# Ten of twelve adaLN modulation vectors: from 512-column matmuls to row sums on three engines

## The chip, the cores and the metric

One Trainium2 chip, one core. The metric is device microseconds (us) of one execution of the whole program; lower is better. Three runs of the kernel before gave 2099.13 us in the median (2097.63 to 2105.65).

## What is computed

Two layers of a diffusion backbone over 512 latent and 256 context tokens of width 1024, all in float32. Before every sub-layer the tokens are normalised and modulated by vectors that depend on the sample alone. Per layer `l` there are six vectors of 1024 numbers (shift, scale and gate of the mixer, then of the experts), each in two variants: from `c` for the latents and from `c_ctx` for the context.

```python
mods  = jnp.split(silu_c  @ ada_w[l] + ada_b[l], 6, axis=-1)   # latents
modsc = jnp.split(silu_cc @ ada_w[l] + ada_b[l], 6, axis=-1)   # context
```

`ada_w[l]` is 1024 x 6144, so one vector (layer `l`, number `m`) needs a 1024 x 1024 block of weights, 4 MB, read once. Twelve such blocks are read in all; the change is about ten of them. After the modulations of a mixer come attention heads, an output projection, a router and 16 experts.

## The kernel before

The weights arrive in tiles with 128 rows of `ada_w` on the 128 partitions. The product with the two silu vectors sums over rows, so over partitions and over eight tiles. `csil` holds the silu vectors as columns: `csil[:, k, 0:2]` belongs to the rows of tile `k`, and 30 further columns are zero.

**Where the modulations are computed.** `ada_first` (L183) makes vectors 0 and 1 of layer 0 at the very start; it isn't changed. The other ten come out of `ada(l, g, ...)` (L217 to L256), five generators that each make two vectors. One has a pool of two 1 MB tiles (`aw`, L403) and loads two tiles ahead (L221, on SP's queue). Each of its eight steps `k` issues four matmuls (L234), with 32 stationary columns and 512 moving columns each, into four quarters of the partitions of one PSUM tile `ps_ada`. After the eighth step VectorE adds the bias (L239), TensorE transposes the row (L244), VectorE copies to `modT` (L248) and makes `Asc` (L252), and GpSimd's queue writes the gates to DRAM (L256).

**How the work is interleaved.** Layer 0's mixer starts with a stage, some 60 to 360 us, in which the projections of the heads (`job`, L516, made of `proj_t`, L474, and `proj_v`, L499), the differential attention (`diff_head`, L651) and the generators of `ada` run together. Generators stand in two queues: `fill` takes the projections, `fill2` takes `ada`. `run_fill(n)` (L612) steps them: every third turn steps `fill2`, the others step `fill`.

- `dense(4); drain()` (L548): the first four projection jobs, q and k of head 0 with 12 steps each, and two value jobs of 24 steps each, 72 steps in all.
- For each of four heads `dense(2)` (24 steps), the `ada` generators of that head (L552), and `diff_head`, whose `weave` makes 26 turns of `run_fill`.
- `dense(2); drain(True)` (L561): two value jobs for the neighbourhood heads, and whatever `ada` has left. Then `st_a.close()` gives `aw`'s memory to the pool `p0n` of the neighbourhood attention (L564).

**What sets the order on an engine.** The program is written in this order, but a planner orders each engine's instructions anew, with earlier code first among what it takes to be ready. A tile of a pool waits for the release of an earlier tile of the same tag. Projections, `ps_ada` and `ps_adat` share the PSUM tag "mm", which has two buffers (L397); scores have the tag "S", transposes "tr", attention outputs "pv". Each engine and each DMA queue (SP's, ACT's, GpSimd's) runs its list in order.

Of the kernel before, what the change touches and what calls it, by code (L numbers as in the profile page):

```python
# [10 lines left out]
F32 = mybir.dt.float32  # L11
# [3 lines left out]
AF = mybir.ActivationFunctionType  # L15
OP = mybir.AluOpType
# [4 lines left out]
D = 1024  # L21
# [107 lines left out]
def _build(tc, a, out, dump=None, upto=99):  # L129
# [6 lines left out]
    with ExitStack() as root:  # L136
# [77 lines left out]
                        ada_ins[8] = V.scalar_tensor_tensor(Asc[0][0][:, v, ks], modT[0][:, 1, v, ks], 1.0, norm_t[:, 0, ks], op0=OP.add, op1=OP.mult)  # L214
                    yield

        def ada(l, g, csil, wp, pp, sm):  # L217

            def load(k):
                w = wp.tile([P, 2048], F32, name="w_ada", tag="w")  # L220
                Y.dma_start(w, a["ada_w"][l, k * P:(k + 1) * P, g * 2048:(g + 1) * 2048])  # L221
                return w

            br = wp.tile([P, 512], F32, name="adab", tag="br", bufs=1)
            bsrc = a["ada_b"][l:l + 1, g * 2048:(g + 1) * 2048]
            S.dma_start(br, bass.AP(bsrc.tensor, bsrc.offset, [[512, 4], [0, 32], [1, 512]]))
            depth = 2
            ws = deque(load(k) for k in range(depth))
            yield
            ps = pp.tile([P, 512], F32, name="ps_ada", tag="mm")  # L230
            for k in range(8):
                w = ws.popleft()
                for j in range(4):
                    T.matmul(ps[32 * j:32 * j + 32, :], csil[:, k, :], w[:, j * 512:(j + 1) * 512], start=(k == 0), stop=(k == 7))  # L234
                if k + depth < 8:
                    ws.append(load(k + depth))
                yield
            row = sm.tile([P, 512], F32, name="mrow", tag="t2k", bufs=T2K)
            V.tensor_tensor(row, ps, br, op=OP.add)  # L239
            yield  # L240
            yield
            pt = pp.tile([P, 4, P], F32, name="ps_adat", tag="mm")
            for c4 in range(4):
                T.transpose(pt[:, c4, :], row[:, c4 * P:(c4 + 1) * P], ident)  # L244
            for c4 in range(4):
                src = pt[:, c4, :].rearrange("p (jh jl q) -> p jh jl q", jh=2, jl=2)[:, :, :, 0:2]
                dst = modT[l][:, 2 * g:2 * g + 2, :, c4::4].rearrange("p m v jl -> p m jl v")
                V.tensor_copy(dst, src)  # L248
            for s in range(2):
                if 1 + 3 * s in (2 * g, 2 * g + 1):  # L250
                    for v in range(2):
                        V.scalar_tensor_tensor(Asc[l][s][:, v, :], modT[l][:, 1 + 3 * s, v, :], 1.0, norm_t[:, 2 * s + l, :], op0=OP.add, op1=OP.mult)  # L252
            if g:
                for half in range(2):
                    j = 2 * (g - 1) + half
                    G.dma_start(garow[l][g - 1, :, half * 512:(half + 1) * 512], row[32 * j:32 * j + 2, :])  # L256

        def rstd_pow(dst, ssq, n):
            G.tensor_scalar(dst, ssq, 1.0 / n, EPS, op0=OP.mult, op1=OP.add)
# [135 lines left out]
        def mix0(st, st_h, wu, stage):  # L395
# [4 lines left out]
            bp = st.enter_context(tc.tile_pool(name="p0b", bufs=1, reuse_waits="tile"))  # L400
            sm = st.enter_context(tc.tile_pool(name="p0s", bufs=2, reuse_waits="tile"))
            st_a = ExitStack()
            aw = st_a.enter_context(tc.tile_pool(name="p0aw", bufs=2, reuse_waits="tile"))  # L403
            csil = lo.tile([P, 8, 32], F32, name="csil", tag="csil")
            S.dma_start(csil, a["cp"])
            S.dma_start(ident, a["ident"])
            S.dma_start(norm_t, a["norm_t"])
            S.activation(csil, csil, AF.Silu)
            hh = hx.tile([P, 8, 768], F32R, name="hh", tag="hh")
            hl = hx.tile([P, 8, 768], F32R, name="hl", tag="hl")  # L410

# [26 lines left out]
                if n == UNIT0:  # L438
                    prep(0)

            with tc.tile_pool(name="p0ax", bufs=2, reuse_waits="tile") as ax:
                first = ada_first(csil, [aw, ax], pp, sm, between)
                for g in range(2):
                    next(first)
                    if g == 0:
                        for i in range(6):
                            S.activation(junk, xt[i], AF.Square, accum_out=ssq[:, i:i + 1])
                        rstd_pow(ssq, ssq, D)
                        for i in range(6):
                            V.tensor_scalar(xt[i], xt[i], ssq[:, i:i + 1], None, op0=OP.mult)  # L450
                    for k in range(4 * g, 4 * g + 4):
                        pt = pp.tile([P, 8, P], F32, name="ps_h", tag="S")
                        for i in range(6):
# [81 lines left out]
            def dense(n):  # L535

                for _ in range(n):
                    fill.append(job(cur[0]))
                    cur[0] += 1


            with tc.tile_pool(name="p0d", bufs=2, reuse_waits="tile") as dp:
                rope = dp.tile([P, 2, LX], F32, name="rope0", tag="rope0", bufs=1)
                with after[0], after[1], after[2]:
                    Y.dma_start(rope, a["rope0"])
                    prep(1)
                rope_of["r"] = rope
                dense(4)  # L548
                drain()
                for h in range(4):  # L550
                    dense(2)
                    for g in (((0, 1),), ((0, 2),), ((1, 0),), ((1, 1), (1, 2)))[h]:  # L552
                        fill2.append(ada(*g, csil, aw, pp, sm))
                    diff_head(h, qk["q", "d", h], qk["k", "d", h], vv, nlam, cT, pp, sm, dp)
                    drain()
                    run_late()
# [46 lines left out]
        def step(q):  # L603
            while q:
                try:
                    next(q[0])
                    return True
                except StopIteration:
                    q.popleft()
            return False  # L610

        def run_fill(n):  # L612

            while n > 0:
                turn[0] += 1
                if turn[0] % 3 == 0:
                    step(fill2)
                elif step(fill):
                    n -= 1
                elif not step(fill2):  # L620
                    return
                else:
                    n -= 2

        def drain(both=False):
            while fill:
# [1158 lines left out]
```

## Time and profile before

| what | value |
|---|---|
| median of three runs | 2099.13 us |
| the profiled execution's own time | 2102.01 us |
| its span, first to last instruction | 2100.2 us |
| busy: TensorE (PE), VectorE (DVE), ScalarE (ACT), GpSimd (POOL) | 93%, 38%, 22%, 11% of the span |
| share of the chain that ended last | PE 79%, DMA 9%, DVE 6% |
| mean granted TensorE clock | 0.976 |

Busy time of PE counts matmuls whose ends are modelled and which overlap one another, so a busy PE is not one at its peak. PEld is the weight load that goes with a matmul. A float32 matmul shows as two records, so four matmuls of a step show as eight. The chain is followed back from the last instruction to what released each step. In rows with `[idle <- X]` the engine stood idle so long before the instruction, until X let it go.

### The profile page before, as it was taken

The numbers are of one execution on the slowest core, as the hardware profiler recorded it, in microseconds if no ns is written. First come the engines' busy times: TensorE is split into PE (matmuls) and PEld (weight loads), VectorE is DVE, ScalarE is ACT, GpSimd is POOL, SyncE is SP. The second block draws the span as 40 slices with busy tenths as digits, with TensorE's granted clock in tenths as the row PEclk, the third lists the DMA queues.
The fourth block names the chain that finished last, engine by engine and source line by source line (L and its number), as shares of the span: only waits on it lengthen the run. The fifth ranks groups of instructions, "written<-read, shape, count | busy, mean of one in ns | idle before, by whom it ended". The sixth has DMA issues, their size and how long they took to land.

```text
span 2100.2 us, 26868 instructions
## 1 busy us (share of the span) xinstructions
PE 1961.1 (93%) x11092; PEld 1044.3 (50%) x11092; DVE 787.7 (38%) x1719; ACT 459.9 (22%) x881; POOL 234.4 (11%) x205
## 2 busy tenths in 40 slices
PE   5899999997979999999999899999969999999997
PEld 1765567875763333333333598455654334443342
DVE  2445553555562322223232741666561121121112
ACT  3233431344330000000000522455320000000002
POOL 1201111112321000000000210101300000000000
PEclk9999999999979999999999999999979999999999
DMA  8354446212667999999999622100278999999965
GB/s 264 121 184 167 171 169 221 64 64 97 216 233 291 355 392 385 397 384 396 386 398 383 175 61 85 66 1 21 106 290 320 389 409 394 375 388 410 388 257 202
DMA packets 174738, 528.81 MB, mean 252 GB/s; under 512 B 11368, under 2 KB 51624, under 8 KB 169496
## 3 DMA queue, kind: packets, MB, share of 16 engines
q1 hardware_dynamic: 162160, 487.75, 61.2%
q0 software_dynamic: 7712, 26.91, 4.6%
q10 hardware_dynamic: 4744, 12.44, 1.9%
q8 instruction: 87, 1.43, 0.3%
q14 instruction: 35, 0.29, 0.0%
HBM read 511.56 MB, written 14.71 MB: 251 GB/s over the span
## 4 chain that ended last, share of the span: by engine, by line
PE 79%; DMA 9%; DVE 6%; ACT 3%; issue 2%; POOL 2%; SPq 0%; ACTq 0%; DVEq 0%; POOLq 0%
DMA moe_w<-in_moe_w 6%; PE ps_a L1125 6%; PE ps_c L173 5%; PE ps_b L1125 5%; PE ps_d L1331 5%; PE ps_d L173 4%; PE ps_a L173 3%; PE ps_b L173 3%; PE ps_x L1318 3%; PE ps_c L1344 3%; PE ps_px L323 3%; PE ps_ada L234 3%; PE ps_e L173 2%; PE ps_px L324 2%; PE ps_px L325 2%; PE ps_s L1737 2%
## 5 line engine op out<-in xcount | busy, mean ns | idle before, releaser
L1125 PE MATMUL ps_b<-moe_w,xeT 128*64 128x512 f32 x512 | 183.2, 597 | 0.0
L1125 PE MATMUL ps_a<-moe_w,xeT 128*64 128x512 f32 x512 | 177.2, 598 | 4.1 <-DVE xeT L1321 3.5
L1127 ACT ACTIVATE hid<-ps_a 128x512 f32<-128x512 f32 x32 | 19.1, 597 | 616.7 <-PE ps_a L1125 401.8
L1128 DVE TENSOR_TENSOR hid<-hid,ps_b 128x512 f32<-128x512 f32 x32 | 22.0, 688 | 313.6 <-PE ps_b L173 149.9
L173 PE MATMUL ps_a<-moe_w,xeT 128*64 128x512 f32 x512 | 139.6, 598 | 0.0
L173 PE MATMUL ps_b<-moe_w,xeT 128*64 128x512 f32 x512 | 137.7, 593 | 0.0
L173 PE MATMUL ps_d<-moe_w,hidT 128*64 128x512 f32 x512 | 114.8, 594 | 3.8 <-DMA moe_w<-in_moe_w 3.6
L173 PE MATMUL ps_c<-moe_w,xeT 128*32 128x512 f32 x1024 | 114.9, 601 | 0.0
L1331 PE MATMUL ps_d<-moe_w,hidT 128*64 128x512 f32 x448 | 102.2, 595 | 0.0
L1125 PEld LDWEIGHTS ps_b<-moe_w,xeT 128*64 128x64 f32 x512 | 54.1, 137 | 74.3 <-issue 68.9
L1125 PEld LDWEIGHTS ps_a<-moe_w,xeT 128*64 128x64 f32 x512 | 51.4, 136 | 77.9 <-issue 71.4
L173 PEld LDWEIGHTS ps_d<-moe_w,hidT 128*64 128x64 f32 x512 | 35.8, 137 | 80.3 <-issue 65.3
L173 PEld LDWEIGHTS ps_b<-moe_w,xeT 128*64 128x64 f32 x512 | 38.9, 137 | 73.4 <-issue 73.1
L1318 PE MATMUL ps_x<-ohT,xhat 128*128 128x128 f32 x512 | 67.8, 296 | 7.2 <-ACT ohT L1311 7.2
L1318 PEld LDWEIGHTS ps_x<-ohT,xhat 128*128 128x128 f32 x512 | 64.8, 209 | 16.3 <-ACT ohT L1311 9.0
L1184 DVE TENSOR_SCALAR xeT<-ps_x,asc,modT 128x64 f32<-128x64 f32 (+1 forms) x256 | 64.5, 321 | 16.4 <-PE ps_x L177 15.7
L1346 DVE TENSOR_TENSOR xacc<-xacc,ps_c 128x512 f32<-128x512 f32 x64 | 44.0, 688 | 70.1 <-PE ps_c L1344 70.1
L173 PEld LDWEIGHTS ps_a<-moe_w,xeT 128*64 128x64 f32 x512 | 37.5, 137 | 65.9 <-issue 63.7
L323 PE MATMUL ps_y<-woh,ch 128*128 128x512 f32 x160 | 66.2, 414 | 3.1 <-ACT ch L861 3.1
L1344 PE MATMUL ps_c<-ye,oh 128*128 128x512 f32 x128 | 65.5, 625 | 1.7 <-DVE ye L1363 1.7
L173 PEld LDWEIGHTS ps_c<-moe_w,xeT 128*32 128x32 f32 x1024 | 32.0, 111 | 70.3 <-issue 68.6
L1331 PEld LDWEIGHTS ps_d<-moe_w,hidT 128*64 128x64 f32 x448 | 37.8, 137 | 55.5 <-issue 54.9
(466 smaller groups left out, 3683.6 us busy)
## 6 DMA issues: line engine op xcount, KB each, us to landing
moe_w<-in_moe_w SPq DMA_DIRECT2D x372, 1024.0 KB, 15.6
w_ada<-in_ada_w SPq DMA_DIRECT2D x40, 1024.0 KB, 4.9
w_in<-in_even_w_in SPq DMA_DIRECT2D x24, 512.0 KB, 3.9
w_ada<-in_ada_w SPq DMA_DIRECT2D x16, 512.0 KB, 9.1
moe_w<-in_moe_w SPq DMA_DIRECT2D x16, 512.0 KB, 11.8
w_in<-in_odd_w_in SPq DMA_DIRECT2D x15, 512.0 KB, 4.5
w_out<-in_even_w_out SPq DMA_DIRECT2D x4, 1024.0 KB
moe_w<-in_moe_w POOLq DMA_DIRECT2D x4, 1024.0 KB, 11.7
```

The costliest lines, as they stand in the source:

```text
L173: return tc.keep_in_program_order(T.matmul(*args, **kw))
L234: T.matmul(ps[32 * j:32 * j + 32, :], csil[:, k, :], w[:, j * 512:(j + 1) * 512], start=(k == 0), stop=(k == 7))
L323: T.matmul(ps, lh, rh, start=first, stop=False)
L324: T.matmul(ps, lh, rl, start=False, stop=False)
L325: T.matmul(ps, ll, rh, start=False, stop=last)
L1125: T.matmul(dst[64 * h:64 * h + 64, :], xt[:, k, :], w[k][:, 512 * h:512 * h + 512], **f)
L1184: V.tensor_scalar(xt[:, k, n0:n1], pt[:, c, n0:n1], Asc[0][1][:, v, k:k + 1], modT[0][:, 3, v, k:k + 1], op0=OP.mult, op1=OP.add)
L1318: T.matmul(pt[:, c, :], xhat[:, i, k * P:(k + 1) * P], ohT[:, i, :], start=(i == 0), stop=(i == 3))
L1331: T.matmul(pd[h][64 * e:64 * e + 64, :], hs[e][:, 2 * q + k, :], w2[e][k][:, 512 * h:512 * h + 512], start=(q + k == 0), stop=(q == 3 and ...
L1344: T.matmul(pc, oh[:, i * P:(i + 1) * P], ye[:, h, :], start=True, stop=True)
L1346: V.tensor_tensor(dst, dst, pc, op=OP.add)
L1737: T.matmul(ps[:, n0:n1], q[e][:, i * P:(i + 1) * P], kk[e][:, n0:n1], start=True, stop=True)
```

## The change

`ada` now makes one vector, so ten generators stand for five. It loads 512 KB tiles (128 x 1024) into a ring of three. For the latent variant ScalarE scales a tile in place by its `csil` column and GpSimd adds the sum so far; for vectors 4 and 5 of layer 1 VectorE does both in one instruction. For the context variant (layer 0, and vectors 0 and 1 of layer 1) VectorE keeps a second sum `a1`, reading the tile before ScalarE overwrites it. What is left to TensorE is the sum over partitions: four matmuls of 256 columns for each variant, with a column of ones. All ten generators are queued before `dense(4)`, and `run_fill` steps `fill2` in two of three turns beside a step of `fill`.

```diff
-        def ada(l, g, csil, wp, pp, sm):
+        def ada(l, m, csil, ones2, wp, pp, sm):
+            nv = 2 if l == 0 or m < 2 else 1
             def load(k):
-                w = wp.tile([P, 2048], F32, name="w_ada", tag="w")
-                Y.dma_start(w, a["ada_w"][l, k * P:(k + 1) * P, g * 2048:(g + 1) * 2048])
+                w = wp.tile([P, D], F32, name="w_ada", tag="w", bufs=3)
+                Y.dma_start(w, a["ada_w"][l, k * P:(k + 1) * P, m * D:(m + 1) * D])
                 return w
...
+            ws = deque((load(0), load(1)))
             yield
-            ps = pp.tile([P, 512], F32, name="ps_ada", tag="mm")
+            prev = None
+            if nv == 2:
+                a1 = wp.tile([P, D], F32, name="a_ada", tag="a", bufs=1)
             for k in range(8):
                 w = ws.popleft()
+                if nv == 2:
+                    if k:
+                        V.scalar_tensor_tensor(a1, w, csil[:, k, 1:2], a1, op0=OP.mult, op1=OP.add)
+                    else:
+                        V.tensor_scalar(a1, w, csil[:, k, 1:2], None, op0=OP.mult)
+                if l and m >= 4:
+                    if k:
+                        V.scalar_tensor_tensor(w, w, csil[:, k, 0:1], prev, op0=OP.mult, op1=OP.add)
+                    else:
+                        V.tensor_scalar(w, w, csil[:, k, 0:1], None, op0=OP.mult)
+                else:
+                    S.activation(w, w, AF.Copy, scale=csil[:, k, 0:1])
+                    if k:
+                        G.tensor_tensor(w, w, prev, op=OP.add)
+                prev = w
+                if k + 2 < 8:
+                    ws.append(load(k + 2))
+                yield
+            br = wp.tile([P, 256], F32, name="adab", tag="br", bufs=1)
+            bsrc = a["ada_b"][l:l + 1, m * D:(m + 1) * D]
+            S.dma_start(br, bass.AP(bsrc.tensor, bsrc.offset, [[256, 4], [0, 32], [1, 256]]))
+            yield
+            ps = pp.tile([P, 256], F32, name="ps_ada", tag="mm")
+            for v, src in enumerate((prev, a1) if nv == 2 else (prev,)):
                 for j in range(4):
-                    T.matmul(ps[32 * j:32 * j + 32, :], csil[:, k, :], w[:, j * 512:(j + 1) * 512], start=(k == 0), stop=(k == 7))
...
+                    T.matmul(ps[32 * j:32 * j + 32, :], ones2[:, 31 - v:63 - v], src[:, j * 256:(j + 1) * 256], start=(v == 0), stop=(v == nv - 1))
+            row = sm.tile([P, 512], F32, name="mrow", tag="t2k", bufs=T2K)[:, 0:256]
             V.tensor_tensor(row, ps, br, op=OP.add)
             yield
             yield
...
+            pt = pp.tile([P, 2, P], F32, name="ps_adat", tag="mm")
...
+            if m in (2, 5):
+                for j in range(4):
+                    G.dma_start(garow[l][m // 3, :, j * 256:(j + 1) * 256], row[32 * j:32 * j + 2, :])
...
-            aw = st_a.enter_context(tc.tile_pool(name="p0aw", bufs=2, reuse_waits="tile"))
+            ones2 = lo.tile([P, 64], F32, name="ones2", tag="ones2")
...
+            aw = st_a.enter_context(tc.tile_pool(name="p0av", bufs=1, reuse_waits="tile"))
...
+                for l, m in [(0, m) for m in range(2, 6)] + [(1, m) for m in range(6)]:
+                    fill2.append(ada(l, m, csil, ones2, aw, pp, sm))
                 dense(4)
                 drain()
                 for h in range(4):
                     dense(2)
-                    for g in (((0, 1),), ((0, 2),), ((1, 0),), ((1, 1), (1, 2)))[h]:
-                        fill2.append(ada(*g, csil, aw, pp, sm))
...
                 turn[0] += 1
-                if turn[0] % 3 == 0:
-                    step(fill2)
-                elif step(fill):
-                    n -= 1
-                elif not step(fill2):
+                more = turn[0] % 3 and step(fill2)
+                if not step(fill) and not more and not step(fill2):
                     return
-                else:
-                    n -= 2
+                n -= 1
```

## Rows read from the trace of the kernel before

**Rows 1.** Busy time by stretch: columns PE, PEld, DVE, ACT, POOL, clock, DMA, GB/s.
```profile
62.00:116.00 54.00, 50.58 (x369) 47.32 (x369) 23.67 (x33) 13.93 (x24) 9.95 (x8) 0.97 0.24 71
116.00:171.00 55.00, 52.99 (x323) 32.92 (x323) 30.25 (x56) 21.11 (x46) 8.25 (x7) 0.97 0.55 188
...
sum 298.00, PE 287.08 PEld 194.68 DVE 146.14 ACT 97.83 POOL 43.26; mean PE 47.85 PEld 32.45 DVE 24.36 ACT 16.31 POOL 7.21
```
**Rows 2.** The chain that ended last, 50 to 380 us: shares by line, and one piece.
```profile
by line: PE ps_ada L234 16.7%; PE ps_s L333 8.3%; PE ps_px L323 6.9%; PE ps_o L697 6.5%; PE ps_px L325 5.0%; PE ps_px L324 5.0%; PE ps_pv L323 4.9%; PE ps_pv L325 4.5%; PE ps_pv L324 4.4%; PE ps_tr L687 3.9%; issue 3.2%; PE ps_pc L323 2.5%;
...
119.87 0.99 PE ps_ada L234 x8
```
**Rows 3.** The tile w_ada, who reads it: ns min/median/max, first and last start.
```profile
L234 PE MATMUL ps_ada<-w_ada,csil x320: 592/593/618, 119.8 to 357.5; 128*32 128x512 f32 x160
...
L221 SPq DMA_DIRECT2D w_ada<-in_ada_w x40: 327/328/429, 52.8 to 351.9; - x40
...
DMA to landing us min/median/max: 4.6/5.2/16.1
```
**Rows 4.** PE in order of time: one row near 61 us.
```profile
60.99 0.51 PE L323 MATMUL ps_px<-hh,wu 128*128 128x512 f32 x1 [1.88 <-DVE hh L461]
```
**Rows 5.** Line L306 from 60 to 361 us: 512 KB loads of projection weights.
```profile
DMA to landing us min/median/max: 3.5/3.8/5.1
```
**Rows 6.** Line L356, one sum of 128x1024 on GpSimd and on VectorE.
```profile
L356 POOL TENSOR_TENSOR wol<-w_out,woh x10: 2348/2440/2920, 489.6 to 1494.8; 128x1024 fp32r<-128x1024 f32 x10
...
L356 DVE TENSOR_TENSOR wol<-w_out,woh x6: 1205/1346/3414, 504.2 to 1495.4; 128x1024 fp32r<-128x1024 f32 x6
```
**Rows 7.** Groups by shape over the whole span, VectorE and ScalarE: busy, mean ns.
```profile
L677 DVE SCALAR_TENSOR_TENSOR dp<-dp,dst 128x768 f32<-128x768 f32 x16 | 16.3, 1018 | 0.5
...
L1668 DVE SCALAR_TENSOR_TENSOR td<-rel,dlg,td 128x896 f32<-128x896 f32 x4 | 4.6, 1143 | 0.0
...
L450 DVE TENSOR_SCALAR xa<-xa,ssq 128x1024 f32<-128x1024 f32 x3 | 2.2, 744 | 22.9 <-POOL ssq L260 22.9
...
L447 ACT ACTIVATE junk<-xa 128x1024 f32<-128x1024 f32 x3 | 3.2, 1051 | 10.5 <-DMA xa<-in_x 10.5
```
**Rows 8.** POOL, then DVE, in order of time around 71 to 81 us.
```profile
71.38 1.29 POOL L486 TENSOR_TENSOR raw<-raw,rope 128x512 f32<-128x512 f32 x1 [3.17 <-DVE sh L485]
73.36 1.29 POOL L488 TENSOR_TENSOR raw<-raw,sh 128x512 f32<-128x512 f32 x1 [0.69 <-DVE sh L487]
78.56 1.79 POOL L486 TENSOR_TENSOR raw<-raw,rope 128x512 f32<-128x512 f32 x1 [3.91 <-DVE sh L485]
...
71.52 1.69 DVE L487 TENSOR_TENSOR sh<-sh,rope 128x512 f32<-128x512 f32 x1
...
78.51 0.69 DVE L487 TENSOR_TENSOR sh<-sh,rope 128x512 f32<-128x512 f32 x1
```
**Rows 9.** PE in order of time near 359 us, then the whole of line L323's ps_pv.
```profile
359.04 0.63 PE L244 MATMUL ps_adat<-ident,mrow 128*128 128x128 f32 x4 [0.59 <-DVE mrow L239]
...
359.74 0.28 PE L325 MATMUL ps_pv<-wh,hl 128*128 128x256 f32 x1
359.86 0.29 PE L323 MATMUL ps_pv<-wh,hh 128*128 128x256 f32 x1
...
L323 PE MATMUL ps_pv<-wh,hh x192: 279/282/390, 79.0 to 384.2; 128*128 128x256 f32 x192
```
**Rows 10.** Groups of instructions from 119 to 361 us: busy us, mean ns, idle before.
```profile
L677 DVE SCALAR_TENSOR_TENSOR dp<-dp,dst 128x768 f32<-128x768 f32 (+1 forms) x24 | 20.2, 840 | 0.8
...
L314 DVE TENSOR_TENSOR wu<-w_in,wu 128x1024 fp32r<-128x1024 f32 x5 | 6.1, 1226 | 1.6 <-ACT wu L313 1.6
...
L314 DVE TENSOR_TENSOR wh<-w_in,wh 128x1024 fp32r<-128x1024 f32 x4 | 4.9, 1222 | 1.2 <-PE ps_pc L325 1.2
```
**Rows 11.** Waits in the DMA queue of SP, whole span: us in total, times, longest.
```profile
SPq L221 <- PE ps_ada L234: 156.0, 38, 10.0
```
**Rows 12.** GpSimd's DMA issues of the gate rows, whole span.
```profile
L256 POOL DMA_DIRECT2D garow<-mrow x8 | 4.3, 538 | 85.8 <-DVE dst L675 68.0 <-DVE mrow L239 17.8
```

More of the change, by code (lines that the diff above doesn't have):

```diff
@@ L215, in ada_first @@
                     yield
-        def ada(l, g, csil, wp, pp, sm):
+        def ada(l, m, csil, ones2, wp, pp, sm):
+            nv = 2 if l == 0 or m < 2 else 1
             def load(k):
-                w = wp.tile([P, 2048], F32, name="w_ada", tag="w")
-                Y.dma_start(w, a["ada_w"][l, k * P:(k + 1) * P, g * 2048:(g + 1) * 2048])
-                return w
[L224 to L228, printed above, removed]
+                w = wp.tile([P, D], F32, name="w_ada", tag="w", bufs=3)
+                Y.dma_start(w, a["ada_w"][l, k * P:(k + 1) * P, m * D:(m + 1) * D])
+                return w
+            ws = deque((load(0), load(1)))
@@ L229, in ada @@
             yield
-            ps = pp.tile([P, 512], F32, name="ps_ada", tag="mm")
+            prev = None
+            if nv == 2:
+                a1 = wp.tile([P, D], F32, name="a_ada", tag="a", bufs=1)
             for k in range(8):
                 w = ws.popleft()
-                for j in range(4):
-                    T.matmul(ps[32 * j:32 * j + 32, :], csil[:, k, :], w[:, j * 512:(j + 1) * 512], start=(k == 0), stop=(k == 7))
-                if k + depth < 8:
-                    ws.append(load(k + depth))
-                yield
@@ L238, in ada @@
-            row = sm.tile([P, 512], F32, name="mrow", tag="t2k", bufs=T2K)
+                if nv == 2:
[12 more added lines that the diff above has]
+                        G.tensor_tensor(w, w, prev, op=OP.add)
@@ L241, in ada @@
             yield
[L242 to L256, printed above, removed]
+            pt = pp.tile([P, 2, P], F32, name="ps_adat", tag="mm")
+            for c2 in range(2):
+                T.transpose(pt[:, c2, :], row[:, c2 * P:(c2 + 1) * P], ident)
+            for c2 in range(2):
+                V.tensor_copy(modT[l][:, m, :, c2::2], pt[:, c2, :].rearrange("p (j r) -> p r j", j=4)[:, 0:2, :])
+            if m in (1, 4):
+                for v in range(2):
+                    V.scalar_tensor_tensor(Asc[l][m // 3][:, v, :], modT[l][:, m, v, :], 1.0, norm_t[:, 2 * (m // 3) + l, :], op0=OP.add, op1=OP.mult)
+            if m in (2, 5):
+                for j in range(4):
+                    G.dma_start(garow[l][m // 3, :, j * 256:(j + 1) * 256], row[32 * j:32 * j + 2, :])
         def rstd_pow(dst, ssq, n):
@@ L408, in mix0 @@
             S.activation(csil, csil, AF.Silu)
+            ones2 = lo.tile([P, 64], F32, name="ones2", tag="ones2")
+            V.memset(ones2, 0.0)
+            V.memset(ones2[:, 31:32], 1.0)
             hh = hx.tile([P, 8, 768], F32R, name="hh", tag="hh")
@@ L439, in between @@
                     prep(0)
-            with tc.tile_pool(name="p0ax", bufs=2, reuse_waits="tile") as ax:
+            with tc.tile_pool(name="p0aw", bufs=2, reuse_waits="tile") as aw, tc.tile_pool(name="p0ax", bufs=2, reuse_waits="tile") as ax:
                 first = ada_first(csil, [aw, ax], pp, sm, between)
```

## The prediction

> **What bounds the kernel now.** I read the page's shares first: TensorE (PE) is busy 93% of the span and holds most of the chain that ended last, so PE's list is the clock of the kernel. Then the stretches of the stage in which `ada` runs: from 62 to 360 us PE is busy 287 of 298 us, DVE 146, ACT 98, POOL 43 [rows 1]. So three engines have room there and PE has none, which is the case for the change. Third, the chain of waits cut to 50 to 380 us: `ps_ada` holds 16.7% of 330 us, 55 us [rows 2]. Last, when `ada` runs and when it could: the loads are issued from 52.8 us on and take at most 16.1 us to land, so the first two tiles lay ready before 70 us; the first of the 160 matmuls starts at 119.8 [rows 3]. Between, PE stood idle, 1.88 us before 60.99 in one row [rows 4], and didn't take them. A load runs far ahead of its place in the program; a matmul into a tile of the tag "mm" doesn't. I read from that that the tiles of a tag are handed out in program order: a later projection can't have a buffer before an earlier `ps_ada` has had its own. The sum rests on this reading.
>
> **What PE loses and gets.** Out go 160 matmuls in 40 steps, 55 us of chain. In come 16 groups (two for each of the six vectors with two variants, one for each of the other four) of four matmuls of 256 columns. A group of 512 columns takes 0.99 us [rows 2]; half the columns cost 0.25 to 0.5, so 4 to 8 us. The transposes stay 20. If PE set the pace afterwards, this would be 47 to 51 us of gain.
>
> **What the others get.** Prices for 128x1024:
> - GpSimd sum: 2.44 us [rows 6]; 8 vectors x 7 = 56 of them, 137 us.
> - VectorE scale-and-add: 1018 ns at 768 columns and 1143 at 896 [rows 7], so 125 ns more for 128 columns and 1.27 us at 1024. With a plain scale of 0.74 for the first step [rows 7], a vector takes 0.74 + 7 x 1.27 = 9.6 us; 6 second variants and 2 vectors of its own make 77 us.
> - ScalarE scale: 1.05 us [rows 7]; 64 of them, 67 us.
>
> None fills its engine alone (137 + 43, 77 + 146, 67 + 98 us in 298), so the busy times would allow the gain. The order of these instructions doesn't.
>
> **The ring of three tiles.** The load for step k+2 takes the buffer of tile k-1, which is read last by the sum of step k. So from the end of one sum to the end of the sum two steps later there lie, one after the other: the load, the second variant's read (ScalarE overwrites the tile, so it waits for VectorE), the scale, the sum. A 512 KB load lands in 3.8 us (3.5 to 5.1) [rows 5]. A hand-over: GpSimd started at 73.36, behind a VectorE row that ended at 71.52 + 1.69 = 73.21 [rows 8], 0.15 us; I take 0.1 for each of five, an estimate.
> - Two variants: 3.8 + 1.27 + 1.05 + 2.44 + 0.5 = 9.1 us for two steps. I add 0.5 because the two engines get into each other's way: VectorE's sum L487 takes 0.69 us at 78.51, but 1.69 when GpSimd began 0.14 us earlier, and GpSimd's L486 takes 1.79 in place of 1.29 when it begins just behind VectorE [rows 8]. So 9.6 for two steps, 38.4 a vector; without the collision 36.4, 12 us less over six vectors.
> - One variant on ScalarE and GpSimd: 3.8 + 1.05 + 2.44 + 0.4 = 7.7, 30.8 a vector.
> - VectorE alone: 3.8 + 1.27 + 0.3 = 5.4, 21.5 a vector.
>
> The sum `a1` has one buffer, and the last tile waits for the final matmuls, so one vector hardly overlaps the next. All ten: 6 x 38.4 + 2 x 30.8 + 2 x 21.5 = 335 us. The memory is that of `ada_first`'s tiles, read until about 58 us, so the first tile lands near 62; with 3 us for the last product, the tenth vector ends at 62 + 335 + 3 = 400. Before, the last `ps_adat` came at 359.04 [rows 9].
>
> The Trainium skill (SBUF — State Buffer, Who interferes with whom) says that a GpSimd instruction and a VectorE one with two SBUF inputs hold one pair of ports in turn, whole instructions long; the trace agrees, 1.69 us in place of 0.69. By this rule the sum is 400, without it 388.
>
> **What waits for the tenth vector.** By the code, 72 projection steps bring 48 steps of `fill2`, and a vector takes 12: four vectors stand inside the first drain. Each head makes 16 more beside its 24 projection steps and 2 alone: 48 + 4 x 18 = 120, all ten vectors. Each asks for two tiles of "mm" between those of the projections, so PE stops at each until the ring is through. The fourth ends near 62 + 4 x 38.4 = 216 us, where the first drain ended at 116. PE's score and transpose tags are free to run ahead, head 0 above all, which makes this cheaper but not quicker: from 216 the heads need 220 us less some 45 of removed `ada`, less what ran ahead, and the other six vectors need 184. So the ring ends last. Behind the tenth stand the two value jobs: 288 matmuls 0.12 us apart [rows 9] are 34 us, less one tile of 3 that has its buffer, 31 us. Before, 25 us of them were left at 359.04 (to 384.2) [rows 9]. So the stage ends (400 - 359) + (31 - 25) = 47 us later. The pool of the neighbourhood heads waits for the same vectors and gives the same 41 us or less.
>
> **Waits on shared engines.** In a head DVE is busy 30 of 55 us and ACT 21 [rows 1]; an `ada` instruction that finds its engine taken waits, and softmax pieces wait behind it. The price is nowhere in the trace. Low end 0, since a wait gives nothing back; high end 0.4 us for each of three instructions in two steps, 0.6 a step, 48 us over 80. I take 8, because in the first four vectors PE's stops leave these engines nearly alone. Together +55 us.
>
> **Edits that I cost at nothing.** 80 loads in place of 40 take SP 0.33 us each [rows 3], 13 us more beside a queue that already waits 156 us for buffers [rows 11]; it will now wait for sums, and projection weights queue behind, inside PE's stops. Gate rows go from 8 to 16 issues at 0.54 us [rows 12], 4 us on GpSimd between vectors. Ten bias loads in place of five and a memset of ones lie beside this. Their cover is the ring's own wait; without it they are worth under 10 us.
>
> **Forecast.** 2102.0 (profiled) + 55 = 2157; the profiled run lies 2.9 above the median of the runs, so 2099.1 + 55, about 2155 us. With 3.5 us loads, 2.35 us sums and no collision a two-variant step pair takes 8.7, and the end lies near 372: +20. With the high wait it is +95. Own range 2119 to 2194.
>
> **The rivals.**
> - *The engines pace it, not the ring.* If loads came early enough, VectorE's and GpSimd's colliding work would remain: 6 x (17.1 + 9.6) + 2 x 17.1 + 2 x 9.6 = 214 us, and the attention's own, 43 [rows 1] + 20 + 11 [rows 10]: 288, from 62 to 350, at most 360 with smaller pieces. Against 352, which by the sum above is no change, that is -2 to +8: 2097 to 2107. For it: such collisions in the rows. Against it: three buffers.
> - *Faster: PE isn't held up.* The mechanism is the end of `ada`'s share of PE's chain, at the two "mm" buffers: 55 - 8 = 47 us, 2052. It decides from a mean of 3.6 us a step downwards, (352 - 62 - 3) / 80, and pays in full under 3.0. For it: GpSimd's 2.44 us is below both, and busy times leave room. Against it: half of 9.6.
> - *In-order lists jam.* Softmax pieces and sums hold each other up at both ends, 0.6 to 1.2 us a step: +95 to +143, 2194 to 2242. For it: DVE would be asked for 223 us in the stage. Against it: the planner sorts each list.
>
> **How the numbers follow.** About 0.5%, 10.5 us, is what a measurement of this kernel can tell from no change. Chances: forecast 0.62, engines 0.13, faster 0.09, jam 0.16. Of the engines' case 0.12 lies within 0.5%, and 0.01 of the faster one: faster 0.08, same 0.13, slower 0.79. The range runs from 2095 to 2210: forecast and engines whole, the lower third of the jam; left out are the faster case and the rest of the jam, 0.19.
>
> **What would show it.** Right: GpSimd sums x56 near 2.4 us; SP waiting at the `w_ada` load for POOL; about 4.8 us from sum to sum in layer 0; the fourth vector's final matmuls near 215 us, the tenth's near 400 to 410; PE busy well under 80% from 80 to 200 us; everything after the stage shifted by one amount. Wrong: projections of head 1 on PE before the fourth vector ends (tiles aren't handed out in order), a spacing under 3.6 us, or the tenth vector before 352.

## The result, and the profile after

The kernel after takes 2198.39 us in the median of four runs (2191.0 to 2200.33), the kernel before beside it 2102.39 (2097.63 to 2109.06): 1.0448 times as long, interval 1.0406 to 1.0489, or 96 us slower. The forecast was about 2155, 55 us slower, in a range from 2095 to 2210. The profiled execution took 2200.33 us with a span of 2198.6, which is 98.4 more than before.

The page first: busy shares, and the granted clock in 40 slices of 55 us.

```profile
PE 1945.5 (88%) x10900; PEld 1067.0 (49%) x10900; DVE 912.3 (41%) x1790; ACT 529.2 (24%) x945; POOL 386.4 (18%) x269
...
PEclk9677678899999799999999999999997999999999
```

TensorE (PE) fell from 93 to 88%, and the clock is down in slices 2 to 8, which are the stage with `ada`. The same stretches as in [rows 1], columns PE, PEld, DVE, ACT, POOL, clock, DMA, GB/s:

```profile
62.00:116.00 54.00, 22.36 (x126) 17.64 (x126) 36.20 (x36) 21.10 (x25) 31.54 (x20) 0.68 0.41 125
116.00:171.00 55.00, 37.08 (x227) 31.08 (x226) 38.50 (x39) 23.43 (x33) 24.83 (x11) 0.76 0.45 136
171.00:226.00 55.00, 32.49 (x217) 28.73 (x218) 34.17 (x43) 21.16 (x36) 28.93 (x12) 0.75 0.44 132
226.00:282.00 56.00, 29.85 (x152) 22.59 (x150) 29.88 (x32) 17.91 (x19) 31.58 (x17) 0.69 0.39 121
```

Before, the last two of these stretches (the first two stand in [rows 1]):

```profile
171.00:226.00 55.00, 52.86 (x314) 32.46 (x312) 30.45 (x62) 20.60 (x45) 9.32 (x8) 1.00 0.54 184
226.00:282.00 56.00, 53.31 (x311) 33.50 (x311) 29.32 (x62) 20.30 (x44) 7.99 (x6) 0.97 0.48 165
```

PE is busy for 41 to 67% of these stretches, where it was busy for 94 to 96%, and no other engine is full either: in the first, VectorE (DVE) stands at 36 of 54 us, GpSimd (POOL) at 32. That is what a chain that goes from engine to engine looks like. Two rows of the waits name its links, the first for PE, the second for SP's DMA queue (us in total, times, longest):

```profile
PE ps_ada L260 <- POOL w_ada L248: 57.7, 7, 29.5
...
SPq L225 <- POOL w_ada L248: 260.9, 55, 10.1
```

The loads wait 55 times for GpSimd's sum to free a tile, and PE waits for the last sum of a vector. PE in order of time at the first vector:

```profile
76.45 0.40 PE L344 MATMUL ps_px<-hh,wu 128*128 128x512 f32 x1
106.30 1.08 PE L260 MATMUL ps_ada<-w_ada,ones 128*32 128x256 f32 x8 [29.45 <-POOL w_ada L248]
107.16 1.08 PE L260 MATMUL ps_ada<-a_ada,ones 128*32 128x256 f32 x8
108.78 0.69 PE L267 MATMUL ps_adat<-ident,mrow 128*128 128x128 f32 x2 [0.55 <-DVE mrow L262]
...
109.69 0.41 PE L344 MATMUL ps_pc<-hh,wu 128*128 128x256 f32 x1
109.91 0.41 PE L342 MATMUL ps_pc<-hh,wu 128*128 128x256 f32 x1
...
110.40 0.28 PE L342 MATMUL ps_pc<-hh,wu 128*128 128x256 f32 x1
110.52 0.28 PE L343 MATMUL ps_pc<-hl,wu 128*128 128x256 f32 x1
```

PE stands 29.45 us in front of the first final matmul, with projections behind it in its list. When it goes on, they start 0.22 us apart at first and 0.12 later; the granted clock is 0.50 from 106.0 to 109.6 us and 1.00 from 110.4 to 112.0. So the stop costs clock too.

Now the ring itself, in the stretch where PE stands and the attention is still: GpSimd, then VectorE, in order of time.

```profile
89.53 2.34 POOL L248 TENSOR_TENSOR w_ada<-w_ada 128x1024 f32<-128x1024 f32 x1 [2.46 <-ACT w_ada L246]
94.32 2.34 POOL L248 TENSOR_TENSOR w_ada<-w_ada 128x1024 f32<-128x1024 f32 x1 [2.45 <-ACT w_ada L246]
99.11 2.34 POOL L248 TENSOR_TENSOR w_ada<-w_ada 128x1024 f32<-128x1024 f32 x1 [2.45 <-ACT w_ada L246]
...
90.97 1.98 DVE L237 SCALAR_TENSOR_TENSOR a_ada<-w_ada,csil,a_ada 128x1024 f32<-128x1024 f32 x1 [2.82 <-DMA w_ada<-in_ada_w]
95.75 1.99 DVE L237 SCALAR_TENSOR_TENSOR a_ada<-w_ada,csil,a_ada 128x1024 f32<-128x1024 f32 x1 [2.80 <-DMA w_ada<-in_ada_w]
```

From sum to sum it is 4.79 us, the predicted 4.8. Each VectorE sum starts while GpSimd's is running (90.97 in 89.53 to 91.87) and takes 1.98 instead of 1.27 us.

How long one holds up the other shows on a short instruction. This one, of six columns, takes 0.17 us at 402.29, where GpSimd makes no sum:

```profile
344.80 2.35 POOL L248 TENSOR_TENSOR w_ada<-w_ada 128x1024 f32<-128x1024 f32 x1 [1.84 <-ACT w_ada L246]
345.14 2.04 DVE L724 SCALAR_TENSOR_TENSOR dst<-dst 128x6 f32<-128x6 f32 x1 [0.48 <-ACT dp L691]
```

It starts inside the sum and ends with it, 347.18 against 347.15. The 2.04 us count as busy time of VectorE. The means over the stage, 60 to 460 us (busy, mean ns):

```profile
L237 DVE SCALAR_TENSOR_TENSOR a_ada<-w_ada,csil,a_ada 128x1024 f32<-128x1024 f32 x42 | 68.8, 1638 | 49.1 <-DMA w_ada<-in_ada_w 48.9
L695 DVE SCALAR_TENSOR_TENSOR dp<-dp,dst 128x768 f32<-128x768 f32 x16 | 22.9, 1432 | 0.3
...
L242 DVE SCALAR_TENSOR_TENSOR w_ada<-w_ada,csil 128x1024 f32<-128x1024 f32 x14 | 17.9, 1277 | 1.0 <-DMA w_ada<-in_ada_w 1.0
...
L248 POOL TENSOR_TENSOR w_ada<-w_ada 128x1024 f32<-128x1024 f32 x56 | 141.1, 2521 | 111.4 <-ACT w_ada L246 103.1
```

L242 runs after GpSimd's last sum: 1277 ns. The same form beside GpSimd takes 1638 (L237), and the softmax piece of 768 columns 1432, where it took 1018 [rows 7].

Where the stage ends, by the tiles (ns min/median/max, first and last start):

```profile
L262 DVE TENSOR_TENSOR mrow<-ps_ada,adab x10: 416/425/426, 108.3 to 448.0; 128x256 f32<-128x256 f32 x10
...
L342 PE MATMUL ps_pv<-wh,hh x192: 274/281/582, 112.5 to 485.1; 128*128 128x256 f32 x192
```

The tenth vector ends at 448.0, its last `ps_adat` starts at 448.9 (359.4 before, and 359.04 for the first of its group [rows 9]); the last value matmul starts at 485.1 (384.2 [rows 9]), 101 us later. The whole program is 98 us longer, so at most 3 us of it are won back later.

### The profile page after: what moved, and what is told of

The parts are those of the page before. It is cut to its first block, busy times and chain, and to the rows that moved or that the text cites. A ratio compares the mean times of both kernels' runs of the same rounds, so it can differ in the third digit from the quotient of the medians.

```text
span 2198.6 us, 26936 instructions
## 1 busy us (share of the span) xinstructions
PE 1945.5 (88%) x10900; PEld 1067.0 (49%) x10900; DVE 912.3 (41%) x1790; ACT 529.2 (24%) x945; POOL 386.4 (18%) x269
## 4 chain that ended last, share of the span: by engine, by line
PE 71%; DVE 10%; DMA 10%; POOL 4%; ACT 3%; issue 2%; SPq 0%; ACTq 0%; DVEq 0%; POOLq 0%
PE ps_a L1143 5%; PE ps_c L173 5%; DMA moe_w<-in_moe_w 5%; PE ps_b L1143 5%; PE ps_d L1349 4%; PE ps_d L173 4%; PE ps_a L173 4%; PE ps_b L173 3%; DMA w_ada<-in_ada_w 3%; PE ps_x L1336 3%; PE ps_c L1362 3%; POOL w_ada L248 2%; PE ps_e L173 2%; PE ps_s L1755 2%; PE ps_px L342 2%
## 5 line engine op out<-in xcount | busy, mean ns | idle before, releaser
L248 POOL TENSOR_TENSOR w_ada<-w_ada 128x1024 f32<-128x1024 f32 x56 | 141.1, 2521 | 111.4 <-ACT w_ada L246 103.1
L246 ACT ACTIVATE w_ada<-w_ada,csil 128x1024 f32<-128x1024 f32 x64 | 73.4, 1149 | 109.9 <-DVE a_ada L237 74.4
L1396 POOL TENSOR_TENSOR xacc<-xacc,xhat 128x512 f32<-128x512 f32 x4 | 5.1, 1269 | 531.2 <-ACT xhat L1385 529.5
L237 DVE SCALAR_TENSOR_TENSOR a_ada<-w_ada,csil,a_ada 128x1024 f32<-128x1024 f32 x42 | 68.8, 1638 | 49.1 <-DMA w_ada<-in_ada_w 48.9
L1190 POOL DMA_INDIRECT xe<-gsrc,gidx x16 | 16.1, 1006 | 365.6 <-PE ps_x L177 348.8
L173 PEld LDWEIGHTS ps_d<-moe_w,hidT 128*64 128x64 f32 x512 | 35.8, 137 | 80.6 <-issue 65.0
```

The lines of the kernel that those rows point to most:

```text
L173: return tc.keep_in_program_order(T.matmul(*args, **kw))
L237: V.scalar_tensor_tensor(a1, w, csil[:, k, 1:2], a1, op0=OP.mult, op1=OP.add)
L246: S.activation(w, w, AF.Copy, scale=csil[:, k, 0:1])
L248: G.tensor_tensor(w, w, prev, op=OP.add)
```

## The experiments

All are edits of the kernel after, unless another is named. Line numbers shift a little between kernels. Times are medians; the kernel before beside them had 2099.74 (first four), 2100.33 (the next four), 2100.96 (e9 to e11) and 2100.79 (e12).

| run | us | ratio to before, interval |
|---|---|---|
| kernel after | 2198.39 | 1.0448 (1.0406 to 1.0489) |
| e1, own PSUM tag | 2209.07 | 1.0537 (1.0504 to 1.0570) |
| e2, queued late | 2207.92 | 1.0519 (1.0485 to 1.0554) |
| e3, one variant | 2157.27 | one execution |
| e4, one variant, ring of 4 | 2126.07 | one execution |
| e5, PE never waits | 2154.55 | 1.0262 (1.0242 to 1.0281) |
| e6, loads only | 2057.95 | 0.9796 (0.9779 to 0.9812) |
| e10, e5 without GpSimd's sums | 2088.52 | 0.9937 (0.9919 to 0.9956) |
| e11, e5 without the second variant | 2116.72 | 1.0063 (1.0040 to 1.0086) |
| e7, all on PE | 2101.71 | 0.9998 (0.9984 to 1.0013) |
| e8, split | 2100.52 | 1.0002 (0.9986 to 1.0018) |
| e9, split, VectorE alone | 2095.03 | 0.9971 (0.9959 to 0.9982) |
| e12, the same, earlier | 2090.93 | 0.9953 (0.9935 to 0.9971) |

**e1: is it the PSUM tag that stops PE?** The tiles of `ada` get a tag of their own; the projections keep one buffer of "mm" instead of two, which is a cost of its own in this run.

```diff
-            ps = pp.tile([P, 256], F32, name="ps_ada", tag="mm")
+            ps = pp.tile([P, 256], F32, name="ps_ada", tag="ada", bufs=1)
...
-            pt = pp.tile([P, 2, P], F32, name="ps_adat", tag="mm")
+            pt = pp.tile([P, 2, P], F32, name="ps_adat", tag="ada", bufs=1)
...
-                px = pp.tile([P, 512], F32, name="ps_px", tag="mm")
+                px = pp.tile([P, 512], F32, name="ps_px", tag="mm", bufs=1)
```

(and the same for `ps_pc` and `ps_pv`.)

> The modulation tiles get a PSUM tag of their own (one buffer) and the projections keep the other buffer; nothing else changes. Theory (the projections stand in line behind modulation tiles of the tag mm): PE runs through the first drain as before, granted clock from 62 to 226 us back above 0.9 (0.68 to 0.76 in the changed kernel), the value jobs no longer wait for the tenth vector; the ten vectors still need their ring, 41 us each for six, so the tenth ends at 400 to 425 and only the memory of the neighbourhood heads waits for it: 2140 to 2170 us. Rival 1 (collisions of VectorE and GpSimd slow the softmax, and that is the cost): within 15 us of the changed kernel, 2185 or more. Rival 2 (only the place in the program matters): back to 2100.

A miss: 2209 us, and the tenth vector ends at 442.0. Rival 1 has the time right; e10 and e11 take up its cause. PE in order of time:

```profile
81.74 0.40 PE L344 MATMUL ps_px<-hh,wu 128*128 128x512 f32 x1
103.60 1.08 PE L260 MATMUL ps_ada<-w_ada,ones 128*32 128x256 f32 x8 [21.47 <-POOL w_ada L248]
```

Projections do run further ahead: from 60 us until the fourth vector ends (230.5 us), 20 `ps_px` matmuls of a kind have run, where the kernel after has 12 until 232, those of head 0 and no more. But PE still stands 54.3 us at the final matmuls, with no tile to wait for. So it is PE's own list: it runs in order, and the final matmul stands in it where the sums aren't done. The tag is one of two things that fix that order, and freeing it doesn't remove the stop. What the tag alone is worth stays open, since the projections lost a buffer in the same edit.

**e2: the ten vectors queued after the first drain.**

```diff
-                for l, m in [(0, m) for m in range(2, 6)] + [(1, m) for m in range(6)]:
-                    fill2.append(ada(l, m, csil, ones2, aw, pp, sm))
                 dense(4)
                 drain()
+                for l, m in [(0, m) for m in range(2, 6)] + [(1, m) for m in range(6)]:
+                    fill2.append(ada(l, m, csil, ones2, aw, pp, sm))
```

> The ten generators are queued after the first drain in place of before it. Theory (one vector at a time through a ring of three, 40 us for each of six): the first drain ends near 116 us again, but the second to tenth vector still follow one another, so the tenth ends at 430 to 450 and the total stays at 2165 to 2200. Rival (queueing four vectors in the first drain is what costs): 2100 to 2125.

2208 us, 8 above the theory's range and far from the rival's. PE is busy for 48.67 of 55 us at a clock of 0.99 from 116 to 171, but the clock falls to 0.70 to 0.85 in the stretches from 171 to 450, and the tenth vector ends at 487.8 instead of 448.0, later than the 430 to 450 expected. PE waits 32.8 us at L260 for GpSimd and 30.0 for VectorE's last sums, together 62.8, where the kernel after had 57.7 for GpSimd. So queueing the vectors early is not the fault; wherever the ring lies, PE comes to its end and stands.

**e5 and e6: PE never waits, and the sums left out.** In e5 the final matmuls read zeros; in e6 L237 to L248 are gone as well.

```diff
-                    T.matmul(ps[32 * j:32 * j + 32, :], ones2[:, 31 - v:63 - v], src[:, j * 256:(j + 1) * 256], start=(v == 0), stop=(v == nv - 1))
+                    T.matmul(ps[32 * j:32 * j + 32, :], ones2[:, 31 - v:63 - v], still, start=(v == 0), stop=(v == nv - 1))
```

> The kernel after, but the 64 final matmuls read a constant tile of zeros instead of the sums, so that nothing on PE waits for the ring; the sums themselves are all made. This leaves out the sum over the partitions, so the modulations are the bias alone. Theory (PE stands in its list at a final matmul until the ring is through, and loses clock while it stands): PE is busy over 46 of 54 us in 62 to 116 (22.4 in the kernel after) at a granted clock over 0.9, the heads are through by about 320 us, and only the memory of the neighbourhood heads then waits for the ring, which still needs 38 to 42 us a vector in layer 0 and ends between 400 and 430. Of the 25 us that stood behind the tenth vector before, the value jobs are then done. So the time is 2102 + (400 to 430 - 359) - 25 = 2118 to 2148, 50 to 80 us below the kernel after. Rival (the sums slow the softmax pieces, and PE would be as late without its stops): 2175 or more, and PE busy under 40 us in 116 to 171.

> As e5_pe_never_waits, and the sums on ScalarE, GpSimd and VectorE are left out too: the 80 loads, the final matmuls on zeros, the new queueing and stepping stay. Theory (what the change takes from PE is worth 47 to 51 us if nothing waits for sums, and queueing, loads and smaller pieces cost nothing): 2045 to 2065. Rival (the new order of the lists or the 80 loads cost something by themselves): 2080 or more. The difference to e5_pe_never_waits is the price of the sums with PE not waiting for them: their collisions with the attention and the late memory.

e6 gives 2057.95, 42 us under the kernel before: that is what PE gains by losing `ada`, with the new queueing and the 80 loads in place. The wrong modulations of these runs don't shorten the rest: behind the last value matmul the program takes 1713.4 us in e6, 1713.5 in the kernel after and 1716.0 before. e5 gives 2154.55, 6.5 above its range: the sums alone cost 97 us over e6 although no PE instruction waits for them directly, and PE's waits for them the other 42 to 44 of the kernel after (42 when each is set against the kernel before beside it). e5's first stretches:

```profile
62.00:116.00 54.00, 42.14 (x277) 36.27 (x277) 40.90 (x44) 20.45 (x26) 32.23 (x19) 0.91 0.47 145
116.00:171.00 55.00, 45.16 (x280) 36.27 (x280) 40.82 (x44) 26.63 (x36) 31.08 (x16) 0.88 0.47 147
```

PE is back at 42 and 45 us from 22 and 37, at a clock of 0.91 and 0.88, less than the 46 expected: now its attention is slow instead. VectorE is busy, its waits for GpSimd included, for 51.20 of 56 us from 226 to 282 and for 51.12 of 54 from 282 to 336. By 232 us 36 `ps_px` have run in place of 12, and still the ring is not through before the last row here starts (tile `w_ada`):

```profile
L225 SPq DMA_DIRECT2D w_ada<-in_ada_w x80: 327/328/433, 58.4 to 431.6; - x80
...
L242 DVE SCALAR_TENSOR_TENSOR w_ada<-w_ada,csil x14: 1274/1284/1286, 394.3 to 435.6; 128x1024 f32<-128x1024 f32 x14
```

The ring ends at 437, later than the 400 to 430 expected. Then the memory of the neighbourhood heads comes free: GpSimd issues their mask at 437.2 us (360.4 in the kernel before), 77 us late. 26 of these are given back, as the value jobs behind the tenth vector are done by then (last start 428.5), and the span is 51 longer than before.

**e10 and e11: which sums cost.** From e5, either GpSimd's sums or VectorE's second variant is left out.

```diff
-                    if k:
-                        G.tensor_tensor(w, w, prev, op=OP.add)
```
```diff
-                if nv == 2:
-                    if k:
-                        V.scalar_tensor_tensor(a1, w, csil[:, k, 1:2], a1, op0=OP.mult, op1=OP.add)
-                    else:
-                        V.tensor_scalar(a1, w, csil[:, k, 1:2], None, op0=OP.mult)
```

> From e5_pe_never_waits (PE reads zeros): GpSimd's 56 sums are left out too, ScalarE's scaling and VectorE's second variant stay. The ring is then 3.8 + 1.28 + 1.15 + 0.3 = 6.5 us for two steps, 26 us a two-variant vector, and ends near 62 + 6 x 26 + 2 x 21 + 2 x 22 = 304 if nothing disturbs it. Theory (GpSimd's sums are what makes VectorE's pieces long): 128x768 pieces under 1150 ns in the mean (1791 in e5_pe_never_waits), a_ada sums under 1350 (1632 there), and 2060 to 2085. Rival (VectorE's 77 us of extra work delay the softmax by themselves): 2105 or more.

> From e5_pe_never_waits (PE reads zeros): VectorE's second variant is left out, GpSimd's 56 sums stay. The ring is 7.7 us for two steps, 31 us a vector for eight and 22 for two, and ends at 351 undisturbed, 375 to 400 with the attention. Theory (VectorE's pieces suffer from GpSimd's sums, and the ring's length from both): 128x768 pieces still over 1300 ns, and 2154 less the 40 to 60 us that the ring is shorter: 2095 to 2120. Rival (the second variant alone is the price): pieces under 1150 ns and 2060 to 2085.

e10 takes 2088.5 (3.5 above the expected range), e11 2116.7. So GpSimd's 56 sums cost 66 us (e5 less e10), the 48 instructions of the second variant 38 (e5 less e11). Together these are 104, more than the 97 of all sums, so the two aren't independent. The same groups of VectorE from 60 to 460 us, first e5:

```profile
L237 DVE SCALAR_TENSOR_TENSOR a_ada<-w_ada,csil,a_ada 128x1024 f32<-128x1024 f32 x42 | 68.6, 1632 | 23.1 <-DMA w_ada<-in_ada_w 23.1
L697 DVE SCALAR_TENSOR_TENSOR dp<-dp,dst 128x768 f32<-128x768 f32 x16 | 28.7, 1791 | 0.1
```

e10:

```profile
L237 DVE SCALAR_TENSOR_TENSOR a_ada<-w_ada,csil,a_ada 128x1024 f32<-128x1024 f32 x42 | 55.3, 1317 | 17.0 <-DMA w_ada<-in_ada_w 16.7
...
L695 DVE SCALAR_TENSOR_TENSOR dp<-dp,dst 128x768 f32<-128x768 f32 x16 | 16.2, 1011 | 0.1
```

e11:

```profile
L692 DVE SCALAR_TENSOR_TENSOR dp<-dp,dst 128x768 f32<-128x768 f32 x16 | 21.5, 1346 | 0.5
```

Without GpSimd's sums the softmax piece is back at 1011 ns and the 1024-column sum at 1317, though VectorE has as much to do. With them and without the second variant the piece still takes 1346. So these VectorE pieces are long because GpSimd is summing, not because VectorE is full. The Trainium skill (SBUF — State Buffer, Who interferes with whom) says that a VectorE instruction with two SBUF inputs and a GpSimd one that reads SBUF shut each other out for whole instructions. The six-column instruction above agrees, as it ends when GpSimd's sum does; the VectorE sum at 90.97 lost a little less, 0.70 us of the 0.90 that GpSimd's still ran.

**e3 and e4: the ring's length.** In e3 every vector has one variant; e4 has a fourth tile as well, in the memory of the second variant's sum. A longer ring wasn't tried on the full kernel.

```diff
-            nv = 2 if l == 0 or m < 2 else 1
+            nv = 1
...
-                w = wp.tile([P, D], F32, name="w_ada", tag="w", bufs=3)
+                w = wp.tile([P, D], F32, name="w_ada", tag="w", bufs=4)
```

(the second pair of lines is e4's alone.)

> Leaves out the context variant of the modulations (VectorE's second sum and its matmuls); ring of three as in the change. Theory: load, scale and sum remain in the loop of two steps, 3.8 + 1.15 + 2.4 + 0.4 = 7.8 us, so 3.9 us from sum to sum in the first vectors (4.8 in the change), a vector in 31 to 33 us, and a total of 2105 to 2140. Rival (the engines' own work sets the pace, not the ring): 2.4 to 2.6 us from sum to sum, a vector in 20 us.

> As the run before it, with four tiles in the ring in place of three (in the memory of the sum that is left out). Theory: the loop now spans three steps, 7.8 / 3 = 2.6 us from sum to sum, near the 2.4 of GpSimd alone; a vector in 21 to 23 us, the tenth ends before the heads do, and PE sets the pace again: 2055 to 2095 us, 30 us or more below the ring of three. Rival (engines, not the ring): the same spacing and the same time as with three tiles.

2157.27 and 2126.07, each from one execution, 17 and 31 us above their ranges, but 31 us apart as expected. In e3 the GpSimd sums stand 7.6 us apart for two steps in quiet stretches, the predicted 7.7. In e4 the second to the fifth vector take 22 to 28 us in place of 30 to 36, later ones up to 48, with the attention's pieces among the sums (the softmax piece 1686 ns in the mean), and PE still waits 24.9 us at L260 for GpSimd. One tile more is worth 31 us; that the rest is the collisions' is only argued.

**e7 and e8: the control, and a split.** e7 sums every vector by matmuls from 512 KB tiles in a ring of four, with the new queueing; e8 does that for the six vectors with two variants only.

```diff
+            pe = nv == 2
...
+                if pe:
+                    for j in range(4):
+                        T.matmul(ps[32 * j:32 * j + 32, :], csil[:, k, :], w[:, j * 256:(j + 1) * 256], start=(k == 0), stop=(k == 7))
```

(e7 has `pe = True`.)

> One vector a generator, the new queueing and stepping, but every vector by matmuls (eight steps of four pieces of 256 columns) from a ring of four 512 KB tiles. Theory (the sums on three engines are what costs): PE has the same 55 us of work as before in twice the pieces, and no ring to wait for, so 2095 to 2115. Rival (queueing all ten vectors ahead of the first projections costs by itself): 2130 or more.

> As e7_all_on_pe for the six vectors with two variants; the four vectors with one variant (layer 1, numbers 2 to 5) are summed as in the kernel after, 16 of 40 us-long steps less on PE, three loads ahead. Theory (a ring of four without the second variant needs 23 to 27 us a vector, and PE's list meets few final matmuls that aren't ready): 20 us less on PE, of which stops give some back: 2080 to 2105. Rival (any sum in the stage costs PE more than it saves): 2110 to 2140, above e7_all_on_pe.

e7 is the kernel before again, 2101.71: queueing, stepping and small loads together cost nothing that shows. e8, at 2100.52, is inside its range, yet gains nothing although four of ten vectors are off PE. GpSimd's 14 sums bring the softmax piece to 1422 ns again (1018 in e7):

```profile
L694 DVE SCALAR_TENSOR_TENSOR dp<-dp,dst 128x768 f32<-128x768 f32 x16 | 22.7, 1422 | 0.3
```

**e9 and e12: VectorE alone, no GpSimd.** From e8: the four one-variant vectors in one VectorE instruction a step, queued by head as in the kernel before.

```diff
-                elif m >= 4:
+                else:
...
+                    for l, m in (((0, 2), (1, 2), (0, 3)), ((0, 4), (1, 3), (0, 5)), ((1, 0), (1, 4)), ((1, 1), (1, 5)))[h]:
+                        fill2.append(ada(l, m, csil, ones2, aw, pp, sm))
```

> From e8_split: the four one-variant vectors are summed by VectorE alone, GpSimd and ScalarE keep out, and the vectors are queued by head as in the kernel before, about one VectorE vector a head. Theory (in e8_split it was GpSimd's sums that slowed VectorE's pieces, 1422 ns in the mean for 128x768 where e7_all_on_pe has 1018, and gave back PE's saving): the pieces stay under 1100 ns, 38 us of VectorE fit beside the attention, and of 16 steps of a little over 1 us most comes out: 2080 to 2095. Rival (VectorE's own queue is the price, whoever else works): 2098 to 2115, pieces near 1018 ns but PE waiting for them.

2095.03, 0.3% under the kernel before and at the upper end of its range, and the softmax piece is at 1013 ns. The edit changes the queueing as well, so how much of the 5 us against e8 comes from leaving GpSimd out isn't shown. PE's largest wait:

```profile
PE ps_ada L255 <- DVE w_ada L241: 15.2, 1, 15.2
```

That is the last vector, with nothing behind it. e12 puts the four vectors earlier, as `((1, 2), (0, 2), (1, 3)), ((0, 3), (1, 4), (0, 4)), ((1, 5), (0, 5)), ((1, 0), (1, 1))`.

> As e9_vector_only_split, with the four VectorE vectors queued earlier: the first at the head of head 0's, none in the last head, where PE then ends with two vectors by matmuls. Theory (PE stood 15.2 us at the last VectorE vector's final matmuls in e9_vector_only_split, at the end of the stage and with nothing else to do): that wait is under 3 us, the granted clock in 336 to 400 is 1.00 (0.87 there), and the time 2075 to 2090. Rival (the wait comes from the ring's order and moves to another place): 2090 to 2105, with a wait of over 8 us for VectorE elsewhere.

2090.93, 0.47% under the kernel before (interval 0.29 to 0.65%) and the lowest median here of a kernel that computes all of the reference; it is 0.9 us above the theory's range. Both gains, 0.3 and 0.47%, lie under the 0.5% that the prediction took as what can be told from no change. The 15 us are gone, and in their place stands this one:

```profile
PE ps_ada L238 <- DMA w_ada<-in_ada_w: 7.1, 7, 2.9
```

The clock in 336 to 400 us is 0.92, not the 1.00 expected: with PE summing at the end, it now waits for loads, and not for VectorE as the rival had it. The intervals of e9 and e12 overlap, so that e12 is the better of the two is not shown.

## Why the prediction was right, and where its sum was short

**What PE loses and gets**: 47 to 51 us if PE paced. e6 measured 42. The sum was a little high, in part because of the final groups: at 303.50 us in e6 a group of 256 columns takes 0.57 us until the next matmul starts, not 0.25 to 0.5, so 16 of them are 9 us where 4 to 8 stood.

**The ring of three tiles.** The mechanism and its price in quiet stretches were right: SP waits 55 times for GpSimd, 4.79 us from sum to sum against 4.8. GpSimd's sum took 2.52 us in the mean (2.44 taken), ScalarE's scale 1.15 (1.05), VectorE's 1.28 where GpSimd is silent (1.27). What was mis-sized is its end. Eight vectors were to take 6 x 38.4 + 2 x 30.8 = 292 us from 62, to 354; they ended at 384.7, 31 us late. The last two took 63 in place of 43. Less the 3 us for the last product that my 400 held, these 31 and 20 are the 48 by which the tenth, at 448, came later than that. By vectors it is 17 us in the first four, 4 in the next two, 10 in the two of one variant and 20 in the last two.

**Waits on shared engines** is therefore the term that failed: 8 us, chosen because PE's stops would leave these engines nearly alone in the first four vectors. Even so the first four took 42.6 us each ((232.5 - 62) / 4) and not 38.4. The high end, 48 us, is what the tenth vector lost. In the last two vectors the wait can be read off. GpSimd makes no sum of `ada` there, and VectorE's sums take 1277 ns and wait 1.0 us in all for a load (L242 above); what keeps them is their place in VectorE's list, behind pieces of the attention that wait for others:

```profile
400.69 1.28 DVE L242 SCALAR_TENSOR_TENSOR w_ada<-w_ada,csil 128x1024 f32<-128x1024 f32 x1
...
403.61 0.96 DVE L689 TENSOR_REDUCE dst<-ps_s 128x1 f32<-128x768 f32 x1 [1.16 <-PE ps_s L352]
...
405.10 1.28 DVE L242 SCALAR_TENSOR_TENSOR w_ada<-w_ada,csil 128x1024 f32<-128x1024 f32 x1
```

From sum to sum that is 4.4 us where 2.7 was taken. Nor do PE's stops excuse the small term: e5 shows that with PE free to run the attention early the ring ends at 437 all the same, since attention pieces and sums then meet more often (1791 ns for the softmax piece, 1432 in the kernel after). So the rival *in-order lists jam*, which began at 2194, names what filled the gap between 2155 and 2198, on top of the ring and not in its place: the result lies 4 us above my forecast's own range and in the first part of that rival's. The whole range holds it because it took in the lower third of this rival. The ring was foreseen; that the time still fell inside the range is in part luck.

**The collision rule.** I charged it 0.5 us for two steps, 12 us over six vectors, and nothing for the attention's pieces; at 90.97 it was 0.70. e10 against e5 prices GpSimd's sums at 66 us; the ring is shorter there too, so that is not the collision alone, and how the 66 divide stays open.

**What waits for the tenth vector.** That PE would run no projection of head 1 before the fourth vector was right (12 `ps_px` until 232 us, those of head 0). The reason given was half right: the tag does hold back projections, as e1 has 20 of them by then, but without it PE stops at the final matmuls all the same. The reading "a matmul into a tile of the tag mm doesn't run ahead" should have been "no matmul runs ahead of one that stands before it in PE's list". Behind the tenth were to be 31 us of value matmuls; it was 485.1 - 448.9 = 36.2, some at the lower clock. The sum (448.9 - 359.4) + (36.2 - 24.8) = 100.9 agrees with the span's 98.4, so the form of the calculation held; its first number was short (41 for 89.5), and its second too (6 for 11.4).

**What I left out** is the clock. Before, the granted clock was 0.97 or more in each stretch of [rows 1]; afterwards 0.68 to 0.76 in four stretches, a mean between PE's two levels, 1.2 and 2.4 GHz. Work that was to be caught up quickly after each stop was caught up more slowly; what that costs by itself no run shows.

**Rivals that fell.** *Faster: PE isn't held up* would have needed a mean of 3.6 us a step; it was (448 - 62) / 80 = 4.8. *The engines pace it* gave 350 us for the end of the work; even without any wait of PE it was 437.

**Edits costed at nothing** (loads, bias loads, queueing) did cost nothing that e7 shows (0.9998, interval 0.9984 to 1.0013).

## What to carry to other kernels

Before work is moved off a full engine, follow one unit of it through the engines that take it, buffers included: with three tiles, 4.8 us a step against 0.7 on TensorE (55 us for 80 such tiles) came from load, second sum, scale and sum in a row, while no engine was full. Then look at who shares what: here GpSimd's sums and VectorE's pieces with two inputs lengthened each other, and taking the four one-variant vectors by one VectorE instruction a step, with GpSimd left out and the other six on TensorE, was the only complete form here with a lower median than the kernel before (e9, e12, 0.3 and 0.47%). And an instruction that ends a long side chain stops its engine's whole list, so it belongs in the list where the chain is surely done.

## What the runs showed that I had not expected

- Work that TensorE never waits for directly can be the larger cost: 97 us for the sums against 42 to 44 for PE's waits at them (e6, e5, kernel after). Letting PE go early moved the attention into the sums, and the ring ended only 11 us sooner (437 against 448).
- In e1 a free tile let projections run 8 matmuls of a kind ahead and the program did not gain; PE stood 54.3 us at L260 in place of 57.7.
- In the collisions VectorE lost more than GpSimd: over the stage GpSimd's sum took 2521 ns in the mean (2340 undisturbed), VectorE's 1638 (1277), the softmax piece up to 3081.
